# A hybrid decoder layer on one core: other tiles and another order of loads where the up half of its MLP meets the down half

## The chip, the cores and the metric

One core of one Trainium2 chip runs the whole layer in one program. The metric is device microseconds (us) of one execution: the median of three runs, 1197.63 before the change. A "profile" here is one further execution with the hardware profiler on. Engines are called PE (TensorE, the matmuls; PEld is its loading of weights), DVE (VectorE), ACT (ScalarE), POOL (GpSimd) and SP (SyncE, which here only issues DMAs: loads from DRAM and stores to it).

## The reference

```python
for l in range(DEPTH):                       # DEPTH = 1, 1024 tokens, D_MODEL = 1024, D_FF = 4096
    h = rms_norm(x, norm1_w[l])
    proj = h @ w_in[l]                       # differential attention and gated DeltaNet, in parallel
    ...
    x = x + mix @ w_out[l]
    h = rms_norm(x, norm2_w[l])
    x = x + jnp.square(jax.nn.relu(h @ w_up[l])) @ w_down[l]
```

The change lies in the last line, the MLP: `h @ w_up` is the up half, the product with `w_down` the down half. All of it is float32.

## The kernel before

**Numbers.** A float32 operand goes through PE as two rounded parts: `hH`, the value cast by ACT to fp32r (line 2293), and `hL`, the rest that DVE takes by subtraction (line 2294). `split` does both; three matmuls (high by high, high by low, low by high; lines 3043 to 3045) stand for one. A split of an operand of 128 x 2048 goes in two pieces of 128 x 1024, `j` 0 and 2.

**Seven products for eight.** Each of the two halves of the MLP is cut in two by tokens and in two by the inner dimension, and of the eight block products only seven are made, from sums and differences of blocks (Winograd's form of Strassen's scheme). In the up half this is done for eight groups g of 512 columns of `w_up`. For each group seven tiles leave for DRAM, `ud1` to `ud7`: the activations (Relu and Square by ACT, `act2`) of the four quarters (named a, b, c, d) and the sums that the down half wants (s3, s4 and others). `put` notes a store and `flush` issues it (line 2563).

**The down half** runs for two halves kg of the hidden dimension. Each has seven products i in the order 1, 5, 6, 3, 7, 2, 4, and each product two steps s. I count the 28 steps as m: m0 and m1 are product 1, m2 and m3 product 5, m4 and m5 product 6, m6 and m7 product 3. A step is 48 matmuls of 128 x 512. Its operands are a tile `ur` loaded back from `ud` (1 MB; `u_raw(m)`, line 3007), and a tile of `w_down` (1 MB in two loads; `dn_raw`, line 2999) in tiles `dw`, by names a, b, d, c. Products 5, 6, 3 and 7 use differences of these weights, which DVE makes (line 3137). Both operands are split into `views`, which lie in the same `hH` and `hL` that held the up half's operands, by turns for even and odd m. At the end of a product `leave` adds four banks of PSUM to the accumulators `acc` (line 3031), which are loaded once from `acc_d` (eight tiles of 512 KB, line 3012); product 1 wants the first four, product 5 the last four.

**Tiles and memory.** The kernel before has four tiles `ur0` to `ur3` for the steps in turn, m on `urs[m % 4]`. `ur0` has its own pool. `ur1` and `ur2` lie where the rounded operands `op` of the up half lay, and are free when its last matmul is done. `ur3` lies where the last group's b, s4, d, c and s3 lay, and is free when their stores have landed. The weights' tiles lie where operands of the up half (`T0`, `T1`, `T2`) lay.

**What sets the order.** PE, DVE and ACT run in the order in which the code is written from line 2948 on (`manual_schedule`). The order of SP's queue is made by the framework's scheduler from dependencies and its own estimate of time; `tc.issue_after(x)` keeps a DMA behind another one. SP issues in order and waits at each DMA until its tile is free and its data is there. It also takes eight semaphores in turn, so that a DMA waits until the one eight ahead of it on the queue has landed.

The seam is the code from line 3068 to 3131: the end of the last group (g = 7) of the up half, with the down half's first loads and splits (`ready`) written between its steps.

Of the kernel before, what the change touches and what calls it, by code (L numbers as in the profile page):

```python
# [9 lines left out]
F32 = mybir.dt.float32  # L10
# [8 lines left out]
P = 128  # L19
# [225 lines left out]
def tile_hymba_layer(  # L245
# [6 lines left out]
    nc = tc.nc  # L252
# [10 lines left out]
    ah = ctx.enter_context(tc.tile_pool(name="ah", bufs=1))  # L263
# [44 lines left out]
    ud = {i: dram.tile([FF // 512, P, 2, 512], F32, name=f"ud{i}") for i in range(1, 8)}  # L308
# [254 lines left out]
    with tc.manual_schedule(engines={T.engine, V.engine, S.engine, G.engine}):  # L563
# [65 lines left out]
        for tb in range(3, NT):  # L629
            for u in range(2):  # L630
                nxt, at = spread_at.get((tb, u), (None, 0))
                z[tb, u] = z_mm(tb, u, *pools[tb], nxt, at)
                if nxt is not None:
# [8 lines left out]
                    last = next(parts)  # L642
# [159 lines left out]
    def put(run, n):  # L802
        return "P", 480.0, run, n, True, True
# [1001 lines left out]
    ready = []  # L1805
# [251 lines left out]
    tiles = list(reversed(range(NT)))  # L2057
# [95 lines left out]
    def outproj():  # L2153
# [27 lines left out]
        def norm2(tb, pos, after):  # L2181
# [28 lines left out]
            if pos < AWAY:  # L2210
                yield kept_at
                keep = kept[tb] = row_tile("kept")
                yield vec(1024)
                V.transpose(keep, both)
                state["away"] += 1
                state["back"] += 1
                yield store(4096)
                nc.sync.dma_start(hn_d[pos], keep)
                yield flow.t + SETTLED
                yield from blocks(keep, hn_d[pos])  # L2220
                keep = kept[tb] = keep.rearrange("p (h k c) -> p h k c", h=2, k=4)
                sl = slice(tb * P, tb * P + P)
                for i in range(2):
                    ks = slice(4 * i, 4 * i + 4)
                    yield act(512)
                    S.copy(hH[:, ks, sl], keep[:, i])
                    yield vec(512)
                    V.tensor_tensor(hL[:, ks, sl], keep[:, i], hH[:, ks, sl].bitcast(F32), ALU.subtract)
                normed_at[pos] = flow.t + flow.HOP
                return  # L2230
# [60 lines left out]
    def split(dst, src):  # L2291

        S.copy(dst[0], src)  # L2293
        V.tensor_tensor(dst[1], src, dst[0].bitcast(F32), ALU.subtract)  # L2294
# [169 lines left out]
    def act2(t, src=None):  # L2464
        S.activation(t, t if src is None else src, AF.Relu)
        S.activation(t, t, AF.Square)
# [83 lines left out]
    def u_tile(g, n):  # L2550
        tag = f"ua{g % 2}" if n == "a" else "ud" if n == "d" else n
        u[g][n] = ups[tag].tile([P, 2, 512], F32, tag=tag, name=tag, bufs=1)
        return u[g][n]
# [6 lines left out]
    def flush(keep):  # L2560
        while len(puts) > keep:
            for d, t in puts.pop(0):
                nc.sync.dma_start(d, t)
# [7 lines left out]
    def rounded(g, i):  # L2571
        early[g, i] = [op_.tile([P, 4, 256], F32R, tag="op", name="op", bufs=5) for _ in range(2)]
        S.copy(early[g, i][0], w[g][CH[i]])  # L2573
# [86 lines left out]
    def plus(dst, src):  # L2660
        V.tensor_tensor(dst, dst, src, ALU.add)
# [313 lines left out]
    g = NG - 1  # L2975
# [9 lines left out]
    lo, hi = slice(0, 512), slice(512, 1024)  # L2985
    ur0 = pools["ur0"].tile([P, 4, 512], F32, tag="ur0", name="ur0")
    urs = [ur0]
    wds = [{} for _ in range(NK)]
# [3 lines left out]
    def dn_raw(kg, n, s):  # L2992
        h, cs = W_AT[n]
        if n == "c":
            t = pools["uc"].tile([P, 4, 512], F32, tag=f"c{s}", name="dw")
        else:
            t = pools["tp"].tile([P, 4, 512], F32, tag=f"T{'abd'.index(n)}{'hl'[s]}", name="dw")
        for g in range(2):
            ins = nc.sync.dma_start(t[:, 2 * g:2 * g + 2], w_dn[:, 2 * kg + s, g, h, :, cs])
        wds[kg].setdefault(n, []).append(t)  # L3000
        return ins

    def u_raw(m):
        if m < len(halves):
            kg, i, s = halves[m]
            g0 = 4 * kg + 2 * s
            return nc.sync.dma_start(urs[m % 4].rearrange("p (g q) t -> p g q t", g=2),
                                     ud[i][g0:g0 + 2].rearrange("g p q t -> p g q t"))

    def load_acc(tbs):  # L3010
        for tb in tbs:
            nc.sync.dma_start(accs[tb], acc_d[tb])

    def split4(dst, src):
        for j in (0, 2):
            split([x[:, j:j + 2] for x in dst], src[:, j:j + 2])

    def ready(s, weights, j):
        v = views[4 * s:][:4]
        dst, src = (v[2:4], wds[0]["a"][s]) if weights else (v[0:2], urs[s])  # L3020
        split([x[:, j:j + 2] for x in dst], src[:, j:j + 2])

    def down(kg, i, flip, out, start, stop, then=None):
        bank = bankB if flip ^ (kg % 2) else bankA
        final = kg == NK - 1 and i == 4
        half, ns = out

        def leave(t):
            tb = t + (4 if half == 0 else 0)
            o = accs[tb][:, ns]  # L3030
            V.tensor_tensor(o, o, bank[t], ALU.add)
            if kg == NK - 1 and i in (2, 3, 7, 4):
                nc.sync.dma_start(out2[tb * P:(tb + 1) * P, ns], o)

        for s in range(2):
            m = halves.index((kg, i, s))
            v = views[4 * (m % 2):][:4]
            seq = [(j, t) for t in (0, 2, 1, 3) for j in range(4)] if final and s else \
                [(j, t) for j in range(4) for t in range(4)]
            for j, t in seq:  # L3040
                sl = slice(t * P, t * P + P)
                s0, s1 = start and s == 0 and j == 0, stop and s == 1 and j == 3
                T.matmul(bank[t], v[0][:, j, sl], v[2][:, j], start=s0, stop=False, skip_group_check=True)  # L3043
                T.matmul(bank[t], v[0][:, j, sl], v[3][:, j], start=False, stop=False, skip_group_check=True)  # L3044
                T.matmul(bank[t], v[1][:, j, sl], v[2][:, j], start=False, stop=s1, skip_group_check=True)  # L3045
                if final and s1:
                    leave(t)
            if s == 0:
                while behind:
                    behind.pop(0)()  # L3050
            upcoming(m + 1)
            if s == 0 and then:
                then()
        if not final:
            behind.extend(lambda t=t: leave(t) for t in range(4))
# [4 lines left out]
    def upcoming(m):  # L3060
        if 1 < m < len(halves):
            kg, i, s = halves[m]
            v = views[4 * (m % 2):][:4]
            split4(v[0:2], urs[m % 4])
            split4(v[2:4], wds[kg][NAMES[i]][s])
            u_raw(m + 4)

    t, x = u[g], X[g % 2]
    u_raw(0)
    for s in range(2):  # L3070
        dn_raw(0, "a", s)
    rounded(g, 4)
    rest(g, 4)
    spread(g)
    plus(t["c"], Y)
    ready(0, True, 0)
    ready(0, True, 2)
    act2(t["c"])
    flush(0)
    puts.append([])  # L3080
# [1 line left out]
        pass  # L3082
    plus(t["d"], x)
    S.copy(u_tile(g, "b"), x)
    ready(0, False, 0)
    V.tensor_tensor(u_tile(g, "s3"), t["a"], t["c"], ALU.subtract)
    put(g, "s3", 7)
    act2(t["d"])
    put(g, "d", 4)
    plus(t["c"], t["d"])  # L3090
    put(g, "c", 5)
    ready(0, False, 2)
    u_raw(4)
    for j in (0, 2):
        ready(1, True, j)
    V.tensor_tensor(t["a"], t["c"], t["a"], ALU.subtract)
# [3 lines left out]
    x = X[1 - g % 2]  # L3100
# [3 lines left out]
    octx.close()  # L3104
    ur = ctx.enter_context(tc.tile_pool(name="ur", bufs=1, **right))
    urs += [ur.tile([P, 4, 512], F32, name=f"ur{i}") for i in (1, 2)]
    u_raw(1)
    for tb in tiles:
        accs[tb] = row_tile("acc")
    plus(t["b"], x)  # L3110
# [4 lines left out]
    put(g, "b", 2)  # L3115
    V.tensor_tensor(u_tile(g, "s4"), t["b"], t["a"], ALU.subtract)
    put(g, "s4", 3)
    u_raw(2)
    load_acc(tiles[:4])
    for s in range(2):  # L3120
        dn_raw(0, "d", s)
    flush(0)
    uctx.close()
    pools["uc"] = tpctx.enter_context(tc.tile_pool(name="uc", bufs=1, **left))
    urs.append(pools["uc"].tile([P, 4, 512], F32, name="ur3"))
    last = u_raw(3)
    u_raw(5)
    with tc.issue_after(last.ins):
        load_acc(tiles[4:])
        for s in range(2):  # L3130
            dn_raw(0, "c", s)
    for kg in range(NK):
        wd = wds[kg]

        def both(dst, l, r):
            for s in range(2):
                V.tensor_tensor(wd[dst][s], wd[l][s], wd[r][s], ALU.subtract)

        def loaded(names):
            if kg + 1 < NK:  # L3140
                for n in names:
                    for s in range(2):
                        dn_raw(kg + 1, n, s)

        down(kg, 1, 0, (0, lo), True, False, lambda: both("b", "b", "a"))
        down(kg, 5, 1, (1, hi), True, False, lambda: both("b", "d", "b"))
        down(kg, 6, 0, (0, hi), False, False)
        down(kg, 3, 1, (0, hi), False, True, lambda: both("a", "b", "a"))
        down(kg, 7, 0, (1, hi), False, False, lambda: both("b", "c", "b"))
        down(kg, 2, 1, (0, lo), True, True, lambda: loaded("a"))  # L3150
        down(kg, 4, 0, (1, lo), False, True, lambda: loaded("bdc"))
# [50 lines left out]
```

## Time and profile before

| | |
|---|---|
| median of three runs (lowest, highest) | 1197.63 us (1195.35, 1198.23) |
| the profiled execution's own time | 1198.07 us |
| its span, first to last instruction | 1196.4 us |
| PE busy | 1180.5 us, 99% |
| PEld, DVE, ACT, POOL busy | 992.9, 899.9, 628.4, 232.9 us |
| mean granted PE clock | 0.997 of full |
| moved by DMA | 196.10 MB, 164 GB/s over the span |

Times in the views count from the start of the span. The up half's last matmul starts at 877.66 us, so the seam is the stretch from about 830 to 930 us. A row of a timeline has start, duration, engine, line, operation, out<-in, and in brackets the engine's idle time before it and what ended it. A row of a group has busy time, mean duration in ns and idle time. Matmuls overlap: each is shown with 0.39 us, and one starts every 0.23 us. Buffer numbers are left out of names in the profile, so `ur` stands for all of them, `s` for s3 and s4.

### The profile page before, as it was taken

What the parts mean: (1) busy time and instruction counts of PE and PEld (TensorE: products, weight loads), DVE (VectorE), ACT (ScalarE), POOL (GpSimd) and SP (SyncE); (2) the same over time, 40 slices, a digit from 0 to 9 for tenths busy, and PEclk for the clock granted to TensorE, in tenths of its full rate; (3) what the DMA queues carried; (4) which work ended last, traced back from release to release, by engine and by line L of the source; (5) the groups of instructions that cost most, each with busy time, mean ns of one, the idle gap of its engine ahead of it and who ended that gap; (6) DMA issues with size and microseconds to landing.
All of it is one profiled execution on the core that took longest, in us unless ns stands there. A gap on an engine that the chain in (4) does not pass through costs nothing.

```text
span 1196.4 us, 17818 instructions
## 1 busy us (share of the span) xinstructions
PE 1180.5 (99%) x6286; PEld 992.9 (83%) x6286; DVE 899.9 (75%) x1677; ACT 628.4 (53%) x1150; POOL 232.9 (19%) x278
## 2 busy tenths in 40 slices
PE   9999999999999999999999999999998999999998
PEld 8988887788888878888888888888876888888887
DVE  7878799567778888877995777777886675674853
ACT  6666646334557766775775465554562333433340
POOL 2323211332223432123120422122100000000000
PEclk9999999999999999999999999999998999999999
DMA  9368644576545585344554344434599366322401
GB/s 355 120 144 194 172 121 99 115 207 197 196 143 176 166 211 130 98 91 145 185 179 155 141 167 168 159 109 173 193 374 348 140 211 210 125 91 103 141 36 70
DMA packets 179617, 196.10 MB, mean 164 GB/s; under 512 B 81528, under 2 KB 134312, under 8 KB 179528
## 3 DMA queue, kind: packets, MB, share of 16 engines
q1 hardware_dynamic: 173688, 181.56, 48.4%
q0 software_dynamic: 5696, 13.41, 3.4%
q8 instruction: 49, 0.80, 0.3%
q14 instruction: 40, 0.33, 0.1%
q10 hardware_dynamic: 144, 0.00, 0.0%
HBM read 132.73 MB, written 62.19 MB: 163 GB/s over the span
## 4 chain that ended last, share of the span: by engine, by line
PE 79%; DVE 8%; DMA 7%; issue 2%; SPq 2%; ACT 2%; POOL 1%; DVEq 0%; ACTq 0%; POOLq 0%
PE X L2414 5%; PE X L2416 5%; PE X L2415 5%; PE X L3044 4%; PE X L3045 4%; PE X L3043 4%; PE ps_o L2010 3%; PE ps_sc L1889 2%; PE ps_op L2167 2%; PE ps_op L2165 2%; PE ps_op L2166 2%; PE Y L2416 2%; PE ps_qk L1713 2%; PE Y L2414 2%; PE Y L3044 2%
## 5 line engine op out<-in xcount | busy, mean ns | idle before, releaser
L2293 ACT CAST hH<-ur 128x1024 fp32r<-128x1024 f32 x56 | 58.4, 1050 | 180.7 <-PE Y L3044 77.4
L2294 DVE TENSOR_TENSOR hL<-ur,hH 128x1024 fp32r<-128x1024 f32 x56 | 67.0, 1220 | 40.0 <-ACT hH L2293 40.0
L3043 PE MATMUL X<-hH 128*128 128x512 f32 x224 | 88.3, 394 | 4.6 <-ACT hH L2293 4.6
L3044 PE MATMUL X<-hL,hH 128*128 128x512 f32 x224 | 88.3, 394 | 0.8 <-DVE hL L2294 0.8
L3045 PE MATMUL X<-hH,hL 128*128 128x512 f32 x224 | 88.1, 393 | 0.0
L1228 PE MATMUL ps_dn<-hH,wH 128*128 128x512 f32 x192 | 76.6, 399 | 0.0
L1229 PE MATMUL ps_dn<-hL,wH 128*128 128x512 f32 x192 | 74.9, 390 | 0.0
L1230 PE MATMUL ps_dn<-hH,wL 128*128 128x512 f32 x192 | 74.9, 390 | 0.0
L2577 DVE TENSOR_TENSOR op<-raw,op 128x1024 fp32r<-128x1024 f32 x44 | 57.9, 1317 | 21.1 <-PE X L2415 16.0
L2294 DVE TENSOR_TENSOR hL<-dw,hH 128x1024 fp32r<-128x1024 f32 x56 | 66.0, 1217 | 1.6 <-ACT hH L2293 1.6
L2573 ACT CAST op<-raw 128x1024 fp32r<-128x1024 f32 x44 | 45.7, 1046 | 34.8 <-DVE raw L2569 22.5
L1835 ACT ACTIVATE pexp<-pexp,mx,small 128x128 f32<-128x128 f32 (+7 forms) x64 | 55.1, 862 | 13.4 <-DVE mx L1855 13.4
L829 DVE SCALAR_TENSOR_TENSOR cy<-cp,pv,cy 128x512 f32<-128x512 f32 x72 | 52.3, 737 | 11.1 <-ACT cy L826 10.7
L2293 ACT CAST hH<-dw 128x1024 fp32r<-128x1024 f32 x56 | 55.9, 1045 | 6.4 <-DMA dw<-in_w_down_dram 3.8
L1334 ACT CAST wH<-wraw 128x512 fp32r<-128x512 f32 x66 | 40.3, 614 | 33.1 <-DMA wraw<-in_w_units_dram 17.3
L3043 PEld LDWEIGHTS X<-hH 128*128 128x128 f32 x224 | 42.7, 191 | 14.0 <-ACT hH L2293 5.1
L1713 PE MATMUL ps_qk<-hH,wH 128*128 128x512 f32 x128 | 53.7, 420 | 0.0
L2165 PE MATMUL ps_op<-wH,hH 128*128 128x512 f32 x128 | 53.2, 415 | 0.0
L3044 PEld LDWEIGHTS X<-hL,hH 128*128 128x128 f32 x224 | 42.6, 190 | 10.2 <-DVE hL L2294 1.3
L1336 DVE TENSOR_TENSOR wL<-wraw,wH 128x512 fp32r<-128x512 f32 x60 | 41.0, 683 | 12.6 <-ACT wH L1334 12.3
L1715 PE MATMUL ps_qk<-hH,wL 128*128 128x512 f32 x128 | 50.2, 392 | 0.0
L2167 PE MATMUL ps_op<-wH,hL 128*128 128x512 f32 x128 | 50.2, 392 | 0.0
(476 smaller groups left out, 3630.8 us busy)
## 6 DMA issues: line engine op xcount, KB each, us to landing
ur<-ud SPq DMA_DIRECT2D x28, 1024.0 KB, 5.0
raw<-in_w_up_dram SPq DMA_DIRECT2D x32, 512.0 KB, 4.1
dw<-in_w_down_dram SPq DMA_DIRECT2D x32, 512.0 KB, 5.8
wraw<-in_w_units_dram SPq DMA_DIRECT2D x38, 256.0 KB, 4.0
ud<-ua SPq DMA_DIRECT2D x16, 512.0 KB, 2.9
ud<-s SPq DMA_DIRECT2D x16, 512.0 KB, 2.8
pka<-park_d SPq DMA_DIRECT2D x32, 192.0 KB, 3.8
xt<-in_x_dram SPq DMA_DIRECT2D x8, 512.0 KB, 10.1
```

The costliest lines, as they stand in the source:

```text
L1228: T.matmul(ps, wh[:, k, cs], hH[:, k, sl], start=(k == 0), stop=False)
L1229: T.matmul(ps, wh[:, k, cs], hL[:, k, sl], start=False, stop=False)
L1230: T.matmul(ps, wl[:, k, cs], hH[:, k, sl], start=False, stop=(k == KB - 1))
L1713: T.matmul(ps, wh[:, k, cs], hH[:, k, sl], start=(k == 0), stop=False)
L2165: T.matmul(ps, hH[:, kk, sl], wh[:, k, :], start=(k == 0), stop=False)
L2293: S.copy(dst[0], src)
L2294: V.tensor_tensor(dst[1], src, dst[0].bitcast(F32), ALU.subtract)
L2414: T.matmul(ps, op[0][:, k, cs], h[0][:, k, :], start=start and k == 0, stop=False, skip_group_check=True)
L2416: T.matmul(ps, op[1][:, k, cs], h[0][:, k, :], start=False, stop=stop and k == 3, skip_group_check=True)
L3043: T.matmul(bank[t], v[0][:, j, sl], v[2][:, j], start=s0, stop=False, skip_group_check=True)
L3044: T.matmul(bank[t], v[0][:, j, sl], v[3][:, j], start=False, stop=False, skip_group_check=True)
L3045: T.matmul(bank[t], v[1][:, j, sl], v[2][:, j], start=False, stop=s1, skip_group_check=True)
```

## The change

The first step m0 gets its activations in two new tiles (`first_u`, named ur4), in the memory of the tags KS0 and KS1, which until then hold operands of the last group's second product. The later steps use the four `ur` tiles one place on: m on `urs[(m - 1) % 4]`, so that m1 has ur0, m2 ur1, m3 ur2 and m4 ur3. m0's operand is rounded directly behind the first weights, ahead of Relu and Square of c and d. The loads are written in another order, and `issue_after` ties several: m3's load behind the weights d, the first accumulators behind m2's load, the others behind m4's, and the weights c are asked for only in product 5 (`second`).

```diff
 def u_raw(m):
-            return nc.sync.dma_start(urs[m % 4].rearrange("p (g q) t -> p g q t", g=2),
+            return nc.sync.dma_start(urs[(m - 1) % 4].rearrange("p (g q) t -> p g q t", g=2),
...
     def ready(s, weights, j):
         v = views[4 * s:][:4]
-        dst, src = (v[2:4], wds[0]["a"][s]) if weights else (v[0:2], urs[s])
-        split([x[:, j:j + 2] for x in dst], src[:, j:j + 2])
+        dst, src = (v[2:4], wds[0]["a"][s]) if weights else (v[0:2], urs[0])
+        split([x[:, j:j + 2] for x in dst], src[:, j:j + 2] if weights or s else first_u[j // 2])
...
-            split4(v[0:2], urs[m % 4])
+            split4(v[0:2], urs[(m - 1) % 4])
             split4(v[2:4], wds[kg][NAMES[i]][s])
-            u_raw(m + 4)
-
+            if m > 5:
+                u_raw(m + 4)
+            else:
+                with tc.issue_after(last.ins):
+                    u_raw(m + 4)
+
+    first_u = [ah.tile([P, 2, 512], F32, tag=tag, name="ur4") for tag in ("KS0", "KS1")]
     t, x = u[g], X[g % 2]
-    u_raw(0)
-    for s in range(2):
-        dn_raw(0, "a", s)
+    dn_raw(0, "a", 0)
+    for q in range(2):
+        nc.sync.dma_start(first_u[q], ud[1][q])
+    dn_raw(0, "a", 1)
+    u_raw(1)
     rounded(g, 4)
     rest(g, 4)
     spread(g)
     plus(t["c"], Y)
-    ready(0, True, 0)
-    ready(0, True, 2)
+    for weights in (True, False):
+        for j in (0, 2):
+            ready(0, weights, j)
     act2(t["c"])
...
     plus(t["d"], x)
     S.copy(u_tile(g, "b"), x)
-    ready(0, False, 0)
     V.tensor_tensor(u_tile(g, "s3"), t["a"], t["c"], ALU.subtract)
...
     put(g, "c", 5)
-    ready(0, False, 2)
-    u_raw(4)
     for j in (0, 2):
         ready(1, True, j)
...
     urs += [ur.tile([P, 4, 512], F32, name=f"ur{i}") for i in (1, 2)]
-    u_raw(1)
...
-    u_raw(2)
-    load_acc(tiles[:4])
-    for s in range(2):
-        dn_raw(0, "d", s)
+    last = u_raw(2)
+    with tc.issue_after(last.ins):
+        load_acc(tiles[:4])
+        for s in range(2):
+            last = dn_raw(0, "d", s)
+    with tc.issue_after(last.ins):
+        u_raw(3)
...
     urs.append(pools["uc"].tile([P, 4, 512], F32, name="ur3"))
-    last = u_raw(3)
     u_raw(5)
+    last = u_raw(4)
     with tc.issue_after(last.ins):
         load_acc(tiles[4:])
-        for s in range(2):
-            dn_raw(0, "c", s)
...
+        def second():
+            both("b", "d", "b")
+            if kg == 0:
+                for s in range(2):
+                    dn_raw(0, "c", s)
...
-        down(kg, 5, 1, (1, hi), True, False, lambda: both("b", "d", "b"))
+        down(kg, 5, 1, (1, hi), True, False, second)
```

In the order of the built programs PE has the same instructions in the same places; ACT and DVE have the same ones in another order at the seam; SP has another order there. The first place is ACT between the last cast for the up half (`op`) and the first product's activations b; `+` is the changed program, and `ur_9450`, `ur_9451` are the two new tiles, `ur_9449` is ur0, `ur_9551` ur1, `dw` weights.

```order
 L2573 CAST op<-raw 128x1024
 L2293 CAST hH<-dw 128x2x512 x2
+L2293 CAST hH<-ur_9450 128x2x512
+L2293 CAST hH<-ur_9451 128x2x512
 L2465 ACTIVATE c<-c 128x1024
 L2466 ACTIVATE c<-c 128x1024
-L3084 COPY b<-X_7225 128x1024
-L2293 CAST hH<-ur_9449 128x2x512
+L3092 COPY b<-X_7225 128x1024
 L2465 ACTIVATE ud<-ud 128x1024
 L2466 ACTIVATE ud<-ud 128x1024
-L2293 CAST hH<-ur_9449 128x2x512
```

Both casts of m0's activations stood behind c, one of them also behind d; now both stand ahead of c. (DVE's rests follow the same order.)

The second place is SP's queue from the loads of the first weights on. Before (`ur_9449` is m0's load, `ur_9551` m1's, `ur_9552` m2's):

```order
L3012 DMA acc<-acc_d 128x1024
L2999 DMA dw<-in_w_down_dram 128x2x512 x4
L2563 DMA ud_124<-ua_9157 128x1024
L3007 DMA ur_9449<-ud_124 128x2x1024
L2999 DMA dw<-in_w_down_dram 128x2x512 x5
L3007 DMA ur_9551<-ud_124 128x2x1024
L2563 DMA ud_127<-ud 128x1024
L2563 DMA ud_130<-s_9499 128x1024
L3007 DMA ur_9552<-ud_128 128x2x1024
L2999 DMA dw<-in_w_down_dram 128x2x512
L2563 DMA ud_128<-c 128x1024
L2999 DMA dw<-in_w_down_dram 128x2x512
```

In the changed program (`ur_9449` is m1's load, `ur_9554` m2's, `ur_9555` m3's; m0's two loads stand four and two rows above the first row):

```order
L2999 DMA dw<-in_w_down_dram 128x2x512 x4
L2563 DMA ud_124<-ua_9157 128x1024
L3007 DMA ur_9449<-ud_124 128x2x1024
L2999 DMA dw<-in_w_down_dram 128x2x512 x4
L2563 DMA ud_130<-s_9505 128x1024
L3007 DMA ur_9554<-ud_128 128x2x1024
L3012 DMA acc<-acc_d 128x1024 x3
L2563 DMA ud_127<-ud 128x1024
L3012 DMA acc<-acc_d 128x1024
L2563 DMA ud_128<-c 128x1024
L2999 DMA dw<-in_w_down_dram 128x2x512 x4
L3007 DMA ur_9555<-ud_128 128x2x1024
```

The acc load left the place ahead of the first weights (three more stood further up, between stores of the group before); m2's load took the place of m1's, and m3's load stands at the end of these rows.

The third place is SP's queue around the load that has to wait for stores, with the semaphores that each row waits for. `DMAHW0` to `DMAHW7` are the eight that SP takes in turn, so the first of them in a row is the DMA eight ahead, and a further one is a DMA whose landing is waited for. Before, where `ur3_9589<-ud5` is m3's load, `ur1` m5's and `ur2` m6's:

```order
L3007 DMA ur1_9551<-ud6_129 128x2x1024 [waits DMAHW3_49,DVE_49]
L2563 DMA ud2_125<-b_9495 128x1024 [waits DMAHW4_49,Activation_49]
L2563 DMA ud3_126<-s4_9569 128x1024 [waits DMAHW5_49,DVE_49]
L3007 DMA ur2_9552<-ud3_126 128x2x1024 [waits DMAHW6_49,DVE_49]
L3007 DMA ur3_9589<-ud5_128 128x2x1024 [waits DMAHW7_49,DMAHW5_49,DMAHW4_49]
```

In the changed program, where `ur2_9555<-ud5` is m3's load, `ur0` m5's and `ur3_9592<-ud6` m4's:

```order
L3007 DMA ur2_9555<-ud5_128 128x2x1024 [waits DMAHW2_49]
L2563 DMA ud6_129<-ua1_9157 128x1024 [waits DMAHW3_49,DVE_49]
L2563 DMA ud2_125<-b_9503 128x1024 [waits DMAHW4_49,Activation_49]
L3007 DMA ur0_9449<-ud6_129 128x2x1024 [waits DMAHW5_49,DVE_49]
L2563 DMA ud3_126<-s4_9571 128x1024 [waits DMAHW6_49,DVE_49]
L3007 DMA ur3_9592<-ud6_129 128x2x1024 [waits DMAHW7_49,DMAHW6_49,DMAHW4_49]
```

Before, m3's load waited for the stores of b and s4 to land; now m4's does, and m3's waits for nothing but its turn.

## The prediction

> **What bounds the kernel now.** I read the page first, then the waits of TensorE, its timeline where it waits, the chain of waits there, and last what the loads do at that place. The page:
>
> ```profile
> span 1196.4 us, 17818 instructions
> PE 1180.5 (99%) x6286; PEld 992.9 (83%) x6286; DVE 899.9 (75%) x1677; ACT 628.4 (53%) x1150; POOL 232.9 (19%) x278
> ```
>
> PE is busy 99% of the span, so a change that adds or removes no matmul can only be worth the gaps in PE's row and what its clock loses after them. From 840 us to the end the waits of PE are three:
>
> ```profile
> PE X L3043 <- ACT hH L2293: 4.6, 1, 4.6
> PE X L3044 <- DVE hL L2294: 0.8, 1, 0.8
> PE Z L3045 <- DVE hL L2294: 0.5, 1, 0.5
> ```
>
> All three are at lines 3043 to 3045, the matmuls of the down half, and name the rounding of their operands (2293 is the cast, 2294 the rest). The timeline of PE shows where (start, duration):
>
> ```profile
> 877.66 0.39 PE L2416 MATMUL X<-T2h,op 128*128 128x512 f32 x1
> 878.09 0.50 PE L3043 MATMUL Z<-hH 128*128 128x512 f32 x1
> 879.35 0.50 PE L3045 MATMUL Z<-hH,hL 128*128 128x512 f32 x1 [0.52 <-DVE hL L2294]
> 900.79 0.39 PE L3043 MATMUL X<-hH 128*128 128x512 f32 x1
> 911.44 0.39 PE L3045 MATMUL X<-hH,hL 128*128 128x512 f32 x1
> 916.48 0.79 PE L3043 MATMUL X<-hH 128*128 128x512 f32 x1 [4.65 <-ACT hH L2293]
> 918.12 0.80 PE L3044 MATMUL X<-hL,hH 128*128 128x512 f32 x1 [0.84 <-DVE hL L2294]
> 931.22 0.39 PE L3043 MATMUL Z<-hH 128*128 128x512 f32 x1
> ```
>
> 877.66 is the last matmul of the up half. Step m0 starts at 878.09, m2 at 900.79, m3 at 916.48, m4 at 931.22. A step is 48 matmuls; from 900.79 to 911.44 are 47 starts, 0.2266 us each, 10.88 us a step. **First stall**: without a wait m0 starts at 877.89 and m2 at 877.89 + 21.75 = 899.64; it starts at 900.79, so 1.15 us are lost. **Second stall**: m4 could start at 900.79 + 21.75 = 922.54 and starts at 931.22, so 8.68 us are lost. Of these 4.81 are the wait for m3's first matmul, 1.41 the one for its second, and the other 2.46 must be clock: the windows below grant 0.57 in 916 to 924. Together 9.83 us. The chain of waits tells what is late:
>
> ```profile
> 867.17 9.79 DMA ur<-ud
> 876.99 1.05 ACT hH L2293
> 893.57 14.17 DMA ud<-s
> 907.79 5.62 DMA ur<-ud
> 913.49 1.05 ACT hH L2293
> 914.57 3.50 DVE hL L2294 x3
> 918.12 0.80 PE X L3044
> ```
>
> and SP's own waits there:
>
> ```profile
> SPq L3007 <- DMA ud<-s: 8.2, 1, 8.2
> ```
>
> m0 waits for its load, issued at 867.17 and landed at 876.96. m3 waits for a load that SP issues only at 907.79, because it waits 8.2 us for the store of s4 to land, at 893.57 + 14.17 = 907.74: m3's tile lies where s4 lay. The load lands at 907.79 + 5.62 = 913.41. The store takes 14 us because the DMA engines are full. Windows of 3 to 8 us (busy PE, PEld, DVE, ACT, POOL; clock, DMA share, GB/s):
>
> ```profile
> 866.00:874.00 8.00, 8.00 (x41) 6.80 (x40) 6.06 (x7) 4.14 (x6) 0.00 (x0) 1.00 1.02 351
> 874.00:880.00 6.00, 5.43 (x23) 3.86 (x22) 3.28 (x4) 5.01 (x6) 0.00 (x0) 1.00 1.00 349
> 888.00:896.00 8.00, 8.00 (x37) 6.63 (x36) 7.15 (x5) 6.47 (x8) 0.00 (x0) 1.00 1.03 411
> 896.00:904.00 8.00, 8.00 (x37) 6.60 (x36) 7.77 (x9) 0.68 (x1) 0.00 (x0) 1.00 1.03 413
> 907.00:910.00 3.00, 3.00 (x15) 2.49 (x14) 0.00 (x0) 0.00 (x0) 0.00 (x0) 1.00 0.49 123
> 916.00:924.00 8.00, 6.68 (x17) 4.93 (x18) 8.00 (x6) 5.27 (x6) 0.00 (x0) 0.57 1.02 360
> ```
>
> The share is full from 866 to past 904, then falls to 0.49 while SP waits. So the seam is bound by the order in which one full queue serves its transfers, and by one reuse of memory. Order can be changed; the bytes stay.
>
> **The change part by part.** The work on PE, DVE and ACT is the same, instruction for instruction; what moves is loads and four roundings.
>
> *m0's operand.* Its load goes into tiles that the last readers leave before the weights' tiles are free, so it no longer stands behind the weights. Its four roundings now run before Relu and Square of c. They follow the second cast of the weights (timeline of ACT and of SP, then groups of the page and of the tile dw: count, us or ns of one):
>
> ```profile
> 871.92 1.05 ACT L2293 CAST hH<-dw 128x1024 fp32r<-128x1024 f32 x1 [1.32 <-DMA dw<-in_w_down_dram]
> 887.13 2.00 ACT L2293 CAST hH<-ur 128x1024 fp32r<-128x1024 f32 x2 [4.20 <-DMA ur<-ud]
> ```
> ```profile
> 860.93 0.32 SPq L3012 DMA_DIRECT2D acc<-acc_d  x1
> ```
> ```profile
> L2293 ACT CAST hH<-ur 128x1024 fp32r<-128x1024 f32 x56 | 58.4, 1050 | 180.7 <-PE Y L3044 77.4
> L2294 DVE TENSOR_TENSOR hL<-ur,hH 128x1024 fp32r<-128x1024 f32 x56 | 67.0, 1220 | 40.0 <-ACT hH L2293 40.0
> ```
> ```profile
> L3137 DVE TENSOR_TENSOR dw<-dw x16: 2280/2282/2285, 892.4 to 1135.2; 128x2048 f32<-128x2048 f32 x16
> ```
>
> The weights' cast ends at 872.97, the two casts of u at 874.9 (1.0 each), their rests on DVE, after that of the weights, at 875.4 and 876.6 (1.2 each). m0 needs the first by 878.3: 1.15 us gained, with 3 us to spare. What it displaces, at 1.05 us for a step of ACT and 1.2 for one of DVE: c is squared by 877.0; DVE adds d by 877.8, ACT copies b and squares d by 880.9; DVE takes c + d, m1's two weight rests, a and b, by 886.9, and m1's first rest by 888.1, where m1 needs it at 888.77 + 0.45. Then b's Relu and Square end at 889.0, s4 at 890.2, line 3137's pair at 894.8, m2's two rests of u and the first of its weights at 898.4, where m2 needs it at 899.87. So 1.1 and 1.4 us are left, and 1.3 more if the weights land earlier, since the acc load at 860.93, right ahead of them, is gone (512 KB are 1.28 us at 411 GB/s). I cost this at nothing: the wait before those casts of m1's operand at 887.13 covers it, which now ends sooner; without that cover it would be the 0.8 us or so by which c, d and b are later.
>
> *m3's operand.* It now lies in a tile of the ur pool that is free when the last up matmul is done, like m1's was, and waits for no store; the tile that does wait goes to m4. It is late only if the queue brings it late. What stood in the queue behind m1's load (landed by 887.1, the cast above) up to the store of s4 is the group of issues from 880 to 894 us:
>
> ```profile
> ur<-ud SPq DMA_DIRECT2D x3, 1024.0 KB, 15.2
> dw<-in_w_down_dram SPq DMA_DIRECT2D x3, 512.0 KB
> ud<-s SPq DMA_DIRECT2D x2, 512.0 KB, 9.1
> ud<-ud SPq DMA_DIRECT2D x1, 512.0 KB, 8.3
> ud<-c SPq DMA_DIRECT2D x1, 512.0 KB, 12.4
> ud<-ua SPq DMA_DIRECT2D x1, 512.0 KB, 14.3
> ud<-b SPq DMA_DIRECT2D x1, 512.0 KB
> ```
>
> 3 + 1.5 + 3 = 7.5 MB in 907.74 - 887.1 = 20.6 us, 2.75 us a MB; at the 413 GB/s of the windows it is 2.54. I take both as bounds. In the new order up to the load of 1 MB that landed at 887.1 there is the same amount without that acc load (the store of s3 stands where a dw load stood), so the load there now, m2's, lands at 885.8 to 887.1. Behind it to m3's load: four acc (2 MB), two stores (1), four dw (2), the load itself (1), 6 MB or 15.2 to 16.5 us: **m3's operand lands at 901.0 to 903.6**. From landing to the second matmul the old chain took 918.12 - 913.41 = 4.7 us; m3 would start at 910.53 and its second matmul at 910.76, so it must land by 906.0. 2.4 to 5 us are left, and the stall of 8.68 us goes.
>
> *m4's operand* is what is late next. Its load waits for the stores of b and s4. Behind m3's load come two stores, a load of 1 MB and the store of s4, 2.5 MB, 6.4 to 6.9 us: s4 lands at 907.4 to 910.5. The load then finds an empty queue, as the old one did, and takes the same 5.62: 913.0 to 916.1. m4 starts at 921.42, needs its second matmul's operand at 921.65, so by 917.0 the load must be there. Between 0.9 and 4 us are left. I take zero, at the edge.
>
> *The eight acc loads.* Four were issued by 860.93, ahead of the full stretch, and now stand in it; that is the 2 MB counted above, 5.1 to 5.5 us for all behind it. If the order did not cover it, m3 and m4 would bear that. They themselves are wanted at about 900 and 922 us, the first four land by 894; the last four stand behind m4's load and land at most 5.5 us after 916.1, at 921.6, and m5, whose operands DVE makes after those adds, starts at 932.3.
>
> *The rest* (the turn of the four tiles, weights c three products earlier than their use) moves loads that are 15 us or more ahead of PE.
>
> Sum: 1.15 + 8.68 = 9.83. The profiled execution took 1198.07 us, 1.67 more than its span, and would take 1188.2; the median of the three runs is 0.44 below it: 1197.63 - 9.83 = **1187.8**.
>
> A rule that speaks against the change: the Trainium skill, "DMA: Bandwidth & Descriptors", section "Where 436 GB/s comes from", says that transfers between HBM and SBUF are held to about 358 GB/s by the memory's side. By it a MB takes 2.93 us, m3's load lands at 904.7 and is in time, m4's at 917.6, and m4 waits 0.6 us: 1188.4. The windows with 411 and 413 GB/s over 16 us disagree with it, so the sum goes by the trace.
>
> **The rivals.**
>
> *m4 waits in its turn.* If the stretch runs like the slowest full window above (349 GB/s, 3.0 us a MB), m3's load lands at 905.1, still in time, s4 at 912.6 and m4's at 918.2, 1.2 us late; at 3.2 us a MB (328 GB/s) it is 3 us. The wait of 0.52 us at 879.35 left the clock at 1.00 in 874 to 880, one of 4.8 us took it to 0.57, so below about 3 us it costs itself alone: 1189 to 1191. For it speaks the thin 0.9 us, against it the 411 and 413. (The Trainium skill, "TensorE: Matmul & The Clock Gate", Part 1, puts the idle time after which the clock halves at about 3.4 us; both waits agree.)
>
> *The queue does not serve in turn.* If up to eight open transfers shared the engines, each would land with the last of its eight: m2's load 3.5 MB later, at 895.4 to 896.7 (needed by 895.2, up to 1.5 us), m3's with the s4 store at 910.5, 3 to 4.5 us late and 2.5 of clock: 6 to 8.5 of the 9.83 come back, 1194 to 1196.3, no change or a trace of gain. Against it: the store issued last, at 893.57, landed last, 14.17 us on.
>
> *Slower.* One thing would do it: the full stretch at a far lower rate, now that weights, accumulators and stores share it. At 4.5 us a MB (233 GB/s) m3's load lands at 914.1, 8.1 us late and 2.5 of clock; s4 lands at 925.4, m4's load at 931.0 against 917.0 + 10.6, 3.4 late: 14.0 lost for 9.83 won, 1201.8. By the same steps it decides from 4.0 us a MB, where 9.7 are lost. No window above is below 349 at a full share.
>
> *It does not do what it says*: m3 could be held by its roundings, not its load. Then about 1196.5 would be left, the first stall alone gone. In the chain ACT takes m3's operand up at 913.49, 0.08 us after it landed, so the load was last; I give it no more than the unseen.
>
> **How the numbers follow.** Both stalls gone 0.60; m4 waits up to 3 us 0.25; not in turn 0.08; slow queue 0.04; something unseen 0.03, which I split. The likeliest is 1187.8. The three runs lie between 1195.35 and 1198.23, so the low end is 1187.8 less that lower spread of 2.3, 1185.5; the high end takes in the second case, 1191.5. A change of 0.3%, 3.6 us, is what a measurement here can tell from none: faster than 1194.0 are the first two cases and a part of the third, 0.87; within it 0.09; slower 0.04.
>
> **What would show it.** Right: no wait at lines 3043 to 3045 from 877 to 925 us, m4's first matmul about 43.8 us after the last up matmul (53.6 now), the clock at 1.00 there, m3's load issued near 889 and landed before 906, m4's issued when the store of s4 lands, near 909. Wrong: a wait at the first matmuls of m1 or m2 (the displaced steps on ACT and DVE mattered), a wait at m4 (rate), one over 3 us at m3 (order of service), or waits above 866 us, which I hold untouched.

## The result, and the profile after

| | before | after |
|---|---|---|
| median of six runs of each (lowest, highest) | 1197.93 us (1195.35, 1198.94) | 1189.26 us (1187.85, 1190.5) |
| ratio of the times, 95% interval | | 0.9928 [0.9916, 0.9941] |
| profiled execution, its span | 1198.07, 1196.4 us | 1190.5, 1188.8 us |
| start of the last up matmul | 877.66 us | 879.97 us |
| from there to the end of the program | 318.71 us | 308.82 us |

The change saves 8.67 us, 7.1 to 10.1 by the interval. The forecast was 9.83 and 1187.8 us, range 1185.5 to 1191.5. From the last up matmul to the end the profiles differ by 9.89 us; the 2.3 us by which the profiled execution came later to that matmul is taken up below. One of the six runs of variation 4 below took 1459.1 us, far slower than any other, and is left out of that variation's median and ratio. The page after:

```profile
span 1188.8 us, 17825 instructions
PE 1178.1 (99%) x6286; PEld 992.3 (83%) x6286; DVE 900.4 (76%) x1677; ACT 629.0 (53%) x1150; POOL 235.2 (20%) x278
```

The list of PE's waits from 840 us to the end, three rows before, is empty now. The timeline of PE at the starts of m0, m2, m3 and m4, behind the last up matmul:

```profile
879.97 0.39 PE L2416 MATMUL X<-T2h,op 128*128 128x512 f32 x1
880.19 0.39 PE L3043 MATMUL Z<-hH 128*128 128x512 f32 x1
...
901.95 0.39 PE L3043 MATMUL X<-hH 128*128 128x512 f32 x1
...
912.83 0.39 PE L3043 MATMUL X<-hH 128*128 128x512 f32 x1
...
923.71 0.39 PE L3043 MATMUL Z<-hH 128*128 128x512 f32 x1
```

m0 follows one pitch behind the last up matmul, m2 to m4 are 10.88 us apart, and m4 starts 43.74 us after 879.97 (53.56 before). Both stalls are gone. In windows of 8 us the granted clock stays at 1.00, but the rate is not the 411 and 413 GB/s of before in all of the stretch:

```profile
890.00:898.00 8.00, 8.00 (x37) 6.64 (x36) 8.00 (x6) 3.65 (x4) 0.00 (x0) 1.00 1.04 406
898.00:906.00 8.00, 8.00 (x37) 6.63 (x36) 4.07 (x6) 0.00 (x0) 0.00 (x0) 1.00 1.02 365
...
918.00:926.00 8.00, 8.00 (x37) 6.60 (x37) 6.70 (x8) 7.11 (x8) 0.00 (x0) 1.00 1.03 416
```

SP's queue with m3's load, the store of s4 and m4's load, the DMA view of the moment in which m3's load is issued (us from issue to landing), and SP's wait:

```profile
893.27 0.64 SPq L3007 DMA_DIRECT2D ur<-ud  x1
...
898.34 0.63 SPq L2563 DMA_DIRECT2D ud<-s  x1
913.16 0.37 SPq L3007 DMA_DIRECT2D ur<-ud  x1
```
```profile
ur<-ud SPq DMA_DIRECT2D x1, 1024.0 KB, 13.6
```
```profile
SPq L3007 <- DMA ud<-s: 14.1, 1, 14.1
```

SP still waits for the store of s4, longer than before (14.1 for 8.2 us), but the load behind that wait is m4's, and PE bears nothing of it. ACT takes up m3's operand at 906.93 and m4's at 918.22, within 0.1 us of the loads' landing at 906.86 and 918.13 (the second row names PE, but the matmuls of m2, which held that place, were done by 913):

```profile
906.93 2.00 ACT L2293 CAST hH<-ur 128x1024 fp32r<-128x1024 f32 x2 [12.23 <-DMA ur<-ud]
...
918.22 2.00 ACT L2293 CAST hH<-ur 128x1024 fp32r<-128x1024 f32 x2 [7.40 <-PE X L3044]
```

### The profile page after: what moved, and what is told of

Its sections match the earlier page's. It is cut to its first block, busy times and chain, and to the rows that moved or that the text cites. A ratio compares the mean times of both kernels' runs of the same rounds, so it can differ in the third digit from the quotient of the medians.

```text
span 1188.8 us, 17825 instructions
## 1 busy us (share of the span) xinstructions
PE 1178.1 (99%) x6286; PEld 992.3 (83%) x6286; DVE 900.4 (76%) x1677; ACT 629.0 (53%) x1150; POOL 235.2 (20%) x278
## 4 chain that ended last, share of the span: by engine, by line
PE 80%; DVE 8%; DMA 5%; issue 3%; SPq 2%; ACT 1%; POOL 0%; DVEq 0%; ACTq 0%; POOLq 0%
PE X L2414 5%; PE X L2416 5%; PE X L2415 5%; PE X L3045 4%; PE X L3043 4%; PE X L3044 4%; PE ps_o L2010 2%; PE Y L3043 2%; PE Z L3043 2%; PE Y L3045 2%; PE Z L3045 2%; PE Y L3044 2%; PE Z L3044 2%; PE ps_op L2167 2%; PE ps_op L2165 2%
## 5 line engine op out<-in xcount | busy, mean ns | idle before, releaser
L1334 ACT CAST wH<-wraw 128x512 fp32r<-128x512 f32 x66 | 40.3, 614 | 32.9 <-DMA wraw<-in_w_units_dram 17.4
L1714 PE MATMUL ps_qk<-hL,wH 128*128 128x512 f32 x128 | 50.0, 391 | 0.0
L2166 PE MATMUL ps_op<-wL,hH 128*128 128x512 f32 x128 | 50.0, 390 | 0.0
```

## The experiments

Since executions differ ahead of the seam, I count times here from the start of the last up matmul of each profile. The landing of a load is that of the last of the 16 engines' parts in the trace's DMA events. The expectations count in the same way.

| kernel | m3's load lands | m4's load lands | m3 starts | m4 starts | end | median of its runs, us |
|---|---|---|---|---|---|---|
| before | 35.75 | 22.52 | 38.82 | 53.56 | 318.71 | 1197.93 |
| after | 26.89 | 38.16 | 32.87 | 43.75 | 308.82 | 1189.26 |
| after, again | 26.60 | 37.82 | 32.87 | 43.75 | 308.84 | 1188.49 |
| 1: ur3 for m3 | 38.10 | 26.91 | 41.17 | 56.01 | 321.10 | 1199.85 |
| 2: own tiles alone | 33.11 | 0.36 | 36.19 | 50.24 | 315.33 | 1194.03 (one) |
| 3: roundings late | 26.00 | 37.25 | 32.87 | 43.75 | 308.83 | 1188.55 (one) |
| 4: acc early | 21.12 | 32.29 | 32.87 | 43.75 | 308.84 | 1187.73 |
| 5: d behind m3's load | 19.74 | 36.72 | 32.87 | 43.75 | 308.84 | 1188.10 (one) |
| 6: 4 and 5 together | 12.41 | 31.87 | 32.87 | 43.75 | 308.82 | 1187.50 |
| 7: six acc first | 28.49 | 39.69 | 32.87 | 44.03 | 309.43 | 1189.74 (one) |
| 8: seven acc first | 29.88 | 39.86 | 32.97 | 45.39 | 310.47 | 1190.72 (one) |
| 9: eight acc first | 31.25 | 41.34 | 34.32 | 48.35 | 313.43 | 1193.28 |

**1: is it the memory of the tile?**

```diff
+    SLOT = (0, 1, 3, 2)
+
     def u_raw(m):
...
-            return nc.sync.dma_start(urs[(m - 1) % 4].rearrange("p (g q) t -> p g q t", g=2),
+            return nc.sync.dma_start(urs[SLOT[(m - 1) % 4]].rearrange("p (g q) t -> p g q t", g=2),
...
-            split4(v[0:2], urs[(m - 1) % 4])
+            split4(v[0:2], urs[SLOT[(m - 1) % 4]])
...
-        u_raw(3)
+        u_raw(4)
...
-    last = u_raw(4)
+    last = u_raw(3)
```

> The changed kernel, but m3 again takes the tile that lies where s4 and b lay (ur3) and m4 the free one (ur2); their two loads are exchanged in the code, the rest stays. Theory (the stall of m3 is the reuse of memory): m3's load is issued only when the store of s4 has landed, about 33 us after the start of the last up matmul, takes 5 us and lands at 38, where it is needed by 28.4: 9.8 us of waiting at m3 and about 2.5 of clock, so 1189.3 + 12.3 = 1201 us, and m4 waits for nothing. Rival (it was the order of the queue alone, or m0's early operand that helped m3 too): m3's wait stays under 3 us and the time is below 1193.

Its PE waits from 840 us on, and SP's wait (lines are two further down than in the changed kernel):

```profile
PE X L3045 <- ACT hH L2293: 8.1, 1, 8.1
PE X L3046 <- DVE hL L2294: 0.8, 1, 0.8
```
```profile
SPq L3009 <- DMA ud<-s: 14.4, 1, 14.4
```

The load landed at 38.10 and the program behind the seam took 12.28 us more, as the first theory had it (12.3). The time is 1199.85 us, ratio to before 1.0019 [1.0008, 1.0031]: with the tile's turn alone undone the rest of the change is a small loss, since m3's load lands 2.35 us later than before, with the accumulators' 2 MB ahead of it, and m0 gains only 1.15. So the turn of the tiles carries the gain at m3.

**2: the own tiles of m0 alone.** The kernel before with this:

```diff
         dst, src = (v[2:4], wds[0]["a"][s]) if weights else (v[0:2], urs[s])
-        split([x[:, j:j + 2] for x in dst], src[:, j:j + 2])
+        split([x[:, j:j + 2] for x in dst], src[:, j:j + 2] if weights or s else first_u[j // 2])
...
+    first_u = [ah.tile([P, 2, 512], F32, tag=tag, name="ur4") for tag in ("KS0", "KS1")]
     t, x = u[g], X[g % 2]
-    u_raw(0)
+    for q in range(2):
+        nc.sync.dma_start(first_u[q], ud[1][q])
```

> The kernel before with one part of the change: m0's activations in the tiles of their own, in the place of the old load in the code. The turn of the other tiles, the order of the roundings and of the other loads stay. Theory (the two stalls are separate): the first stall of 1.15 us is gone, since the load alone was late, the second of 8.7 us stays, so 317.6 us from the last up matmul to the end (318.71 before, 308.82 after). Rival (without the new order of roundings and loads the early tiles bring nothing, or what m0 gains m3 loses again): 318.5 to 318.8.

It took 315.33, so neither was right: 3.38 us gained. The waits of PE from 840 us on:

```profile
PE X L3043 <- ACT hH L2293: 1.3, 1, 1.3
PE X L3044 <- DVE hL L2294: 1.1, 1, 1.1
PE Z L3045 <- DVE hL L2294: 0.5, 1, 0.5
PE Z L3043 <- ACT hH L2293: 0.5, 1, 0.5
```

m0 no longer waits, but between m0's start and m2's 1.65 us are lost at the two waits of 0.5 (the list counts from the end that is shown for the matmul before, 0.39 us behind its start, and matmuls start every 0.23): m1's load lands at 10.70 (9.45 before), and m1, due at 11.11, wants its cast of 1.05 us ahead of that. In the kernel before m1 was due later by what m0 lost. So m0's stall had covered another one, and at m2 the first part's gain is gone (23.64, before 23.13). What was gained lies at m3: ur0 no longer holds m0's operand, so m4's load was issued in the old place of m0's, 10.49 us ahead of the last up matmul, not 6.84 behind it. With that 1 MB out of the full stretch the store of s4 landed at 28.08 for 30.08, m3's load at 33.11 for 35.75, so m3 starts 2.63 us earlier than before; the other 0.7 us is nearly all clock, one stretch of 3.41 us at half clock for two, of which a part had passed in waiting (windows in the last section). The two stalls are not separate; they share the queue.

**3: the place of m0's roundings.** The changed kernel with

```diff
-    for weights in (True, False):
-        for j in (0, 2):
-            ready(0, weights, j)
+    for j in (0, 2):
+        ready(0, True, j)
...
     S.copy(u_tile(g, "b"), x)
+    ready(0, False, 0)
...
     put(g, "c", 5)
+    ready(0, False, 2)
```

> The changed kernel, but m0's activations are rounded at the two old places, one piece behind the copy of b and one behind the Square of d; its loads stay in the new tiles. Theory of the prediction (the first stall of 1.15 us came from the late load): with the load already there, the late rounding alone costs little, a wait of 0.3 to 0.5 us at m0's second or third kind of matmul, because ACT reaches the second piece only behind d. Rival (the place of the roundings is what decides, the new tiles add nothing): the whole 1.1 us is back at m0. In both the stall at m3 stays away, and the stretch from the last up matmul to m4's first is 43.8 + what m0 waits.

No wait at all, 308.83; neither the 0.3 to 0.5 us of the first theory nor the 1.1 of the rival. ACT's timeline (the last up matmul is at 878.00):

```profile
875.16 1.05 ACT L2293 CAST hH<-ur 128x1024 fp32r<-128x1024 f32 x1
876.10 1.06 ACT L2465 ACTIVATE ud<-ud 128x1024 f32<-128x1024 f32 x1
877.20 1.06 ACT L2466 ACTIVATE ud<-ud 128x1024 f32<-128x1024 f32 x1
878.17 1.03 ACT L2293 CAST hH<-ur 128x1024 fp32r<-128x1024 f32 x1
```

The second piece is cast only behind m0's start, and PE comes to it later still. The load's arrival was the first stall; the new place of the roundings adds nothing to the time.

**4 to 6: margins.** 4 leaves the first four accumulator loads free, 5 puts the weights d behind m3's load, 6 does both. The edit of 6:

```diff
     last = u_raw(2)
+    load_acc(tiles[:4])
     with tc.issue_after(last.ins):
-        load_acc(tiles[:4])
-        for s in range(2):
-            last = dn_raw(0, "d", s)
+        last = u_raw(3)
     with tc.issue_after(last.ins):
-        u_raw(3)
+        for s in range(2):
+            dn_raw(0, "d", s)
```

> The changed kernel, but the first four accumulator loads (2 MB) are free to go ahead of the full stretch again, as before the change. Theory (in the full stretch only the 2 MB in the queue count, and there is room for them): m3's load lands about 5 us earlier, 21 to 22 us after the start of the last up matmul instead of 26.9, m4's 33 instead of 38.2, and the time is that of the changed kernel, 1189.3 us within 0.1%, since PE waits for neither. Rival (the accumulator loads slow the stretch in a way that PE's waits do not show, or their early place takes engines from the loads of the up half): a time that differs by over 1 us, with waits of PE ahead of the seam.

> The changed kernel, but the four loads of the weights d stand behind m3's load instead of ahead of it. The question is why 6 MB took 17.4 us there, 2.89 us a MB and not the 2.54 to 2.75 of the prediction. Theory A (the loads of weights are slow themselves): m3's load lands 19.6 to 20 us after the start of the last up matmul, 7 us earlier than in the changed kernel (26.9), and the weights behind it still take 7 us for 2 MB. Theory B (something else in that stretch, such as the instruction fetch 17.5 us after that matmul, holds up one of the 16 engines): m3's load lands at about 21.8, spread over its engines as the weights were, and the weights take 5 to 5.5 us for 2 MB. The time stays 1189.3 us in both, as long as the weights d land by about 27.

> The two variations with the widest margins together: the first four accumulator loads free to go early, and the weights d behind m3's load. m3's load should land about 12 us after the start of the last up matmul (9.7 for m2's, and 1 MB more at 2.5 us) instead of 26.9, and m4's at about 32 instead of 38.2. Theory (PE waits for nothing behind 840 us, so margins are worth nothing): 308.8 us from the last up matmul to the end, the time that of the changed kernel within 0.1%. Rival (the 1.3 us by which the variation with early accumulators was faster in its runs than the changed kernel in its own is real): 1.3 us faster here too.

The landings moved as expected (21.12, 19.74, 12.41), and all three end at 308.82 to 308.84. The ratios to before are 0.9921 [0.9901, 0.9941] for 4 and 0.9926 [0.9914, 0.9938] for 6, against 0.9928 [0.9916, 0.9941]: the same time. The medians of 4 and 6 are 0.8 to 1.8 us below the two of the changed kernel, inside these intervals, and PE shows nothing behind the seam that could give it. What they buy is room: m3's load can be up to 15.9 us early (28.34 less 12.41) instead of 1.4.

On the question of 5, windows of the changed kernel from m2's landing to the stores of d and c (3 MB of accumulators and stores), from there to the weights' landing (2 MB), and on to m3's (1 MB):

```profile
889.48:897.01 7.53, 7.53 (x35) 6.23 (x34) 7.53 (x5) 4.10 (x4) 0.00 (x0) 1.00 1.03 412
897.01:904.29 7.28, 7.28 (x34) 6.03 (x33) 5.06 (x7) 0.00 (x0) 0.00 (x0) 1.00 1.02 351
904.29:906.85 2.56, 2.56 (x13) 2.13 (x12) 0.00 (x0) 0.00 (x0) 0.00 (x0) 1.00 1.02 419
```

2.51 us a MB, then 3.64, then 2.56. In 5, the 3 MB, m3's load (1 MB) and the weights (2 MB):

```profile
887.19:894.73 7.54, 7.54 (x35) 6.24 (x34) 7.54 (x6) 4.11 (x4) 0.00 (x0) 1.00 1.02 417
894.73:897.26 2.53, 2.53 (x13) 2.08 (x12) 2.24 (x2) 0.00 (x0) 0.00 (x0) 1.00 1.04 390
897.26:903.02 5.76, 5.76 (x27) 4.79 (x26) 4.68 (x6) 4.00 (x4) 0.00 (x0) 1.00 1.04 377
```

Ahead of the weights m3's load comes at full pace although the instruction fetch (the program's own code, one packet of 16 KB, 1.07 us, at 17.9) falls into its stretch, and the weights behind it took 5.76 us. The loss goes with the weights, as theory A has it, but not with its 7 us, and theory B is not ruled out. A load has landed when the last of its 16 parts has, so a fetch that holds up an engine ahead of the last one does not show in the landing. By these parts the four loads of the changed kernel landed 1.27, 2.24, 2.31 and 1.46 us apart. The middle of the 16 parts took 6.09 of the 7.28 us, so the last one fell back by 1.2 us more, and a fetch of 1.07 us stands at 17.5, in the second of the four. Over the profiles the pace of four such loads in a row goes from 3.70 us a MB (1, right behind 16.9) to 2.66 (8, right behind 20.8). The trace has their packets at 2 KB and 84 ns in the median, those of the other transfers at 4 KB and 159 ns; for 16 engines that is 390 against 412 GB/s, 2.69 and 2.54 us a MB. This explains the lower end. In the slow stretch the 2 KB packets are longer, 107 ns in the mean for 86 ahead of it. What takes the pace up to 3.7 in some places stays open.

**7 to 9: where the margin at m3 ends, and what a short wait costs.** Six, seven and eight accumulator loads ahead of the weights d and m3's load. The edit of 7 (8 and 9 have 7 and 8 in place of 6):

```diff
-        load_acc(tiles[:4])
+        load_acc(tiles[:6])
...
-        load_acc(tiles[4:])
+        load_acc(tiles[6:])
```

> The changed kernel with six accumulator loads instead of four ahead of the weights d and of m3's load, 1 MB more. Two questions: where the margin at m3 ends, and what a short wait costs. With four, m3's load landed 26.9 and 26.6 us after the start of the last up matmul, with eight at 31.25, so with six about 28.8 to 29.2, 0.4 to 0.8 late. Theory A (a wait of this size costs itself alone, as the prediction had it below 3 us): 309.2 to 309.7 us from the last up matmul to the end (308.82 without a wait). Theory B (with eight, two waits of 1.3 and 1.1 us were followed by 3.4 us at half clock; any waits close together do that): 1.7 us more, 310.9 to 311.4.

> The same with seven accumulator loads ahead, 1.5 MB more: m3's load should land at 29.9 to 30.3, 1.5 to 1.9 us late. Its first matmul would wait 0 to 0.5 us and its second the 1.4 us that the rest behind the cast takes. Theory A (waits of under 3 us cost themselves alone): 310.3 to 310.8 us from the last up matmul to the end. Theory B (they are followed by one stretch of 3.4 us at half clock, which costs 1.7): 312.0 to 312.5.

> The changed kernel with all eight accumulator loads ahead of the weights d and of m3's load, 2 MB more in front of it. The question is how wide the margin at m3 is: its load landed 26.9 us after the start of the last up matmul and may land at 28.4. Theory (the queue serves in turn, 2.5 to 2.9 us a MB, and the operand's landing is all that m3 waits for): it lands at 31.9 to 32.7, m3 waits 3.5 to 4.3 us, and 2.5 more if the clock falls as it did in the kernel before; the store of s4 and m4's load move by as much, so m4 waits another 0 to 1 us if the clock holds and less if it falls: 312.3 to 315.6 us from the last up matmul to the end, 1191 to 1195. Rival (landing order is not what decides, or the queue gives room in between): no wait at m3, 308.8.

Six land the load at 28.49, earlier than expected, and cost 0.61 us, 0.3 each within m3 and m4: the edge is near the forecast's 906.0, which is 28.34 here. Seven land it 1.54 late and cost 1.65, the wait alone. PE's timeline and the clock around it:

```profile
911.51 0.50 PE L3043 MATMUL X<-hH 128*128 128x512 f32 x1
913.14 0.50 PE L3044 MATMUL X<-hL,hH 128*128 128x512 f32 x1 [1.13 <-DVE hL L2294]
```
```profile
910.50:913.90 3.40, 2.27 (x9) 1.42 (x8) 3.40 (x4) 1.90 (x3) 0.00 (x0) 1.00 0.25 102
913.90:917.30 3.40, 3.40 (x16) 2.79 (x16) 3.40 (x3) 0.00 (x0) 0.00 (x0) 1.00 0.81 253
```

Theory A holds for one wait. Eight land it 2.91 late, and 4.61 are lost:

```profile
911.80 0.49 PE L3043 MATMUL X<-hH 128*128 128x512 f32 x1 [1.29 <-ACT hH L2293]
913.44 0.50 PE L3044 MATMUL X<-hL,hH 128*128 128x512 f32 x1 [1.14 <-DVE hL L2294]
```
```profile
911.33:914.74 3.41, 1.79 (x7) 1.27 (x8) 3.41 (x4) 1.37 (x2) 0.00 (x0) 1.00 0.14 55
914.74:918.15 3.41, 3.41 (x10) 2.63 (x9) 3.41 (x2) 0.00 (x0) 0.00 (x0) 0.50 0.94 311
918.15:922.00 3.85, 3.85 (x19) 3.18 (x18) 2.77 (x3) 3.08 (x4) 0.00 (x0) 1.00 1.03 421
```

m3 starts 1.45 late, its second matmul 1.41 more, and then PE has half its clock for 3.41 us, 10 matmuls where 3.4 us held 16 above: 1.7 us. The sum is 4.57. Neither wait is longer than 1.3 us. The load came 0.65 us ahead of the range expected and m3 lost 2.86 us by waiting, not 3.5 to 4.3; the end lies in the range expected all the same. The time is 1193.28 us, ratio 0.9967 [0.9955, 0.9979].

**The changed kernel again, for the 2.3 us ahead of the seam.**

> The changed kernel once more. Its first profile has the end of the program 308.82 us behind the last up matmul (318.71 in the kernel before, so 9.89 us gained), but that matmul itself 2.3 us later (879.97 against 877.66), a loss that arises in the first 40 us of the program, where both kernels are the same. Theory (the start differs from execution to execution): the last up matmul lies elsewhere this time, between 877 and 880, the 308.8 us behind it stay within 0.1, and the median of the runs is nearer to 1187.8 than to 1189.3. Rival (the change costs 2 us ahead of the seam): the last up matmul at about 880 again, the median at 1189 to 1190.

The end is 308.84 behind the last up matmul, which itself lies at 879.57: by this profile alone the rival stands. The median, 1188.49 us, lies between the two, with a ratio of 0.9928 [0.9915, 0.9941]. Six variations (1, 3, 5, 7, 8, 9) have the same instructions up to the seam, and there the matmul starts between 877.48 and 878.57; in 4 it is 877.08, in 6 876.26, in 2 876.96. Most of the difference is there early: the 251st matmul of PE comes at 39.92 us before, at 41.76 and 42.23 in the two profiles of the changed kernel and between 39.97 and 40.73 in the nine variations. So with the same instructions executions differ there by some 2 us, and I read the 2.3 us as that. The two profiled executions were also the longest of their groups of runs (1190.5 and 1190.12 us). But both profiles of the changed kernel lie at the late end, so that the changed kernel itself loses up to 2 us there is not excluded.

## Why the prediction was right, and where not

**Sum.** 1.15 + 8.68 = 9.83 was forecast, 9.89 is what the two profiles show from the last up matmul on. The measured 8.67 lies under it; 9.83 is inside the interval, and I read the rest as what executions differ by ahead of the seam. The sum does not test the queue's pace: it is the same for every pace at which both loads come in time, and the pace was forecast too fast. The signs named for being right came: no wait, clock at 1.00, and in the clock of the profile before m3's load issued at 891.0 and m4's at 910.9 (near 889 and 909 were named).

**First stall.** Right in size. Its cause was the load (3), so the step "Its four roundings now run before Relu and Square of c" moved work that did not have to move. That what it displaces costs nothing was right, with more room than the 1.1 and 1.4 us forecast. DVE's timeline after, with m1's rests and m2's rests of u and weights:

```profile
886.94 2.35 DVE L2294 TENSOR_TENSOR hL<-ur,hH 128x1024 fp32r<-128x1024 f32 x2
...
894.79 2.35 DVE L2294 TENSOR_TENSOR hL<-ur,hH 128x1024 fp32r<-128x1024 f32 x2
897.06 2.36 DVE L2294 TENSOR_TENSOR hL<-dw,hH 128x1024 fp32r<-128x1024 f32 x2
```

m1's first rest ends at 888.16, 8.2 us behind the last up matmul, where 10.4 was forecast, in the main because the first weights landed 1.4 us earlier. 2 adds what the prediction did not see: with m1's load left where it was, a wait at m1 takes the first stall's place.

**Second stall.** Right, and by the mechanism named (1). The edge for m3's load, 906.0, held to 0.2 us: in 7 it landed 0.15 behind that, and m4 started 0.28 late.

**The queue's pace** is the term that was mis-sized. In the clock of the profile before (877.66 for the last up matmul) m2's load landed at 887.2 (forecast 885.8 to 887.1), m3's at 904.5 (901.0 to 903.6), the store of s4 at 910.8 (907.4 to 910.5), m4's load at 915.8 (913.0 to 916.1, at the edge 917.0). The 6 MB took 17.4 us, 2.90 a MB, outside 2.54 to 2.75. Those bounds came from stretches in which the weights' loads stood among others; four of them in a row took 3.64 a MB here, though not in every variation. m4's load took 4.97 us in the empty queue, not 5.62; with 5.62 it would have come at 916.5, still ahead of the edge. The margins left were 1.4 us at m3, where 2.4 to 5 was forecast, and 1.2 at m4, inside the 0.9 to 4.

**The rivals.** m4 did not wait; with 1 MB more in the stretch it does, by 0.3 us (7). The queue serves in turn: in the seam loads and stores land in the order of issue in every profile. (By the prediction's own bounds that rival's low ends would be 894.7 for m2's load and 1.4 us late for m3's, not 895.4 and 3.) The stretch was not slow in the sense of the third rival, 2.90 us a MB against the 4.0 from which it decides. The change does what it says (1). The price in the first rival, that a wait below about 3 us "costs itself alone", is wrong where two follow each other (9, and 2): there it costs 1.7 us more. With it that rival would have read 1189 to 1193.

**The rule on 358 GB/s** of the Trainium skill ("DMA: Bandwidth & Descriptors", section "Where 436 GB/s comes from") would have had m3's load at 904.7, and it came at 904.5; m4's at 917.6, and it came at 915.8. It is not that limit that did it: 412 to 419 GB/s passed right ahead of and behind the weights.

## What to carry to other kernels

A tile that a late operand is loaded into should lie in memory that only engines leave, not in memory that a store has to leave, when the queue is full: the reuse cost 12.3 us in the changed kernel (1), and handing that tile to the next step cost nothing. Before one stall is removed, look at which loads it covers, and leave room for the stretch of a full queue: 2 MB of weights took from 5.3 to 7.4 us in it. Two short waits of PE in a row can cost more than their sum.

## What was not expected of the hardware

In the four profiles that have half clock at the seam it comes in whole multiples of 3.41 us, and a gap of that length is not needed for it. The windows over them, before (6.83, twice 3.41), 1 (10.24, three times) and 2 (one); that of 9 is shown above:

```profile
916.27:923.10 6.83, 5.78 (x13) 4.21 (x14) 6.83 (x5) 4.61 (x6) 0.00 (x0) 0.50 1.02 353
```
```profile
915.32:925.56 10.24, 6.03 (x13) 4.42 (x14) 8.78 (x6) 7.64 (x8) 0.00 (x0) 0.50 1.07 406
```
```profile
915.18:918.60 3.42, 3.42 (x10) 2.65 (x9) 3.42 (x3) 1.20 (x2) 0.00 (x0) 0.50 1.11 377
```

The Trainium skill, "TensorE: Matmul & The Clock Gate", Part 1, gives the gate a window of 3413 ns that runs freely; the lengths agree. It lets the clock fall after an idle window, and 9 differs: in the 3.41 us ahead of the half clock PE was shown busy for 1.79, with 7 matmuls, and 8, with 2.27 in a stretch of that length around its wait, kept its clock. How little work is enough to lose the clock is not shown: two cases do not give a threshold, and in 8 the place of the window is not known.
